# The end of a decoder layer: two expert tiles combined on chip instead of three, row pairs summed by GpSimd, five token tiles finished from PSUM

## The chip, the cores and the metric

The kernel runs on one core of a Trainium2 chip. The metric is the device time of one execution in microseconds (us). The core has five engines: TensorE (PE: matmuls, and PEld for its weight loads), VectorE (DVE), ScalarE (ACT), GpSimd (POOL), and SP, whose queue here issues most DMAs. Each runs its own instructions in program order and waits for the others through semaphores. SBUF is the working memory on chip; matmuls write into PSUM, eight banks of 128 rows by 512 fp32 words.

## What is computed

A decoder layer on 1024 tokens of width 1024: attention, then a mixture of 32 experts in which every token goes through two, then an RMS normalization. Only the end matters here:

```python
y = jnp.zeros_like(xt)
for e in range(N_EXPERTS):
    he = jax.nn.silu(xt @ w_gate[e]) * (xt @ w_up[e])
    y = y + combine[:, e:e + 1] * (he @ w_down[e])     # two nonzero weights per token
...
    x = x + y.reshape(B, T, D)
return _rmsnorm(x, final_norm)
# _rmsnorm(x, g) = x * rsqrt(mean(x * x) + 1e-6) * g
```

## The kernel before

**Experts.** The loop `for e in range(NE)` runs 32 jobs. Job `i = 4q + c` is one expert; the four jobs of group `q` share three row tiles of 128 gathered token rows, `x0`, `xq`, `x1` (numbers `j = 3q, 3q+1, 3q+2`), where `xq` is shared by two experts. A job takes two halves of gate and up projection (`gate_up`, 12 matmuls each, on weights that ACT and DVE split into a high and a low part, `split_half`, L98), the activation (`act_mul`), a transposition (`trans_h`), the down projection (`project`, four matmuls into two `s` banks) and the addition of its result to the row tiles (`add`, DVE). `finish(i)` does the last two and, if `c` is above 0, row tile `j` is complete: for `j < 21` GpSimd scatters its rows into `Y_d` (`scatter`), a table in DRAM with two rows per token, one for each of its experts. The down projection of job `e - 1` runs in the round of job `e`. The order on TensorE, ACT, DVE and GpSimd is the order in which the code is written.

**The last group.** The three row tiles of `q = 7` (j = 21, 22, 23) are not scattered. `finish` splits each into a high and a low part (`yk`, appended to `kept`), and `combine_kept` adds them to a token tile's PSUM banks: one matmul per half, part and kept tile with a one-hot matrix (`hots`, made on DVE by `token_onehot`) that sends each kept row to its token. Job 29's `finish` runs in the round of 31, after the first half of its gate and up; job 28's in round 29.

**The final stage.** `load_y` loads the eight token tiles with both rows per token (`fy`, 1 MB each) through SP's queue; the loads wait for the last scatter. `second_rows(t)` lets ACT copy a tile's second rows into two PSUM banks, `combine_kept` adds the kept rows there, and DVE adds the banks to the first rows (L1070). ACT squares the tile and sums the squares (L1075), takes the root (L1082); DVE takes the reciprocal (L1054) and multiplies by it and by the gain (L1057), and SP stores the tile (L1059). Tile `t - 1` is closed (`finish_out`) after tile `t`'s adds; copies run two tiles ahead, over three pairs of banks. The last tile is squared in two halves (L1080) and its sums added (L1081). Since PSUM banks are written by ACT and then added to by TensorE, a bank that has not been opened by a matmul is first written by one (L1043).

The main lines of the stage:

```python
combine_kept(t, early[t], range(NK - 1 if t < EC else 0, NK))
if t + 2 < NT:
    early[t + 2] = second_rows(t + 2, yys[t + 2])
for n, bk in enumerate(early.pop(t)):
    nc.vector.tensor_tensor(o[:, c], o[:, c], bk, op=ALU.add)
if t:
    finish_out(t - 1)
nc.scalar.activation(yy[:, 1, :], o, AF.Square, accum_out=ss)
```

After it the program reads a count of overflowing experts and, where it is zero, ends.

## Time and profile before

| | |
|---|---|
| median of three timed runs | 1029.95 us (1028.26 to 1030.7) |
| the profiled execution | 1027.5 us |
| its span | 1025.7 us |
| mean granted TensorE clock | 0.994 |
| busy, share of the span | PE 96%, DVE 74%, ACT 61%, GpSimd 10% |
| HBM traffic | 206 GB/s over the span |

The page of a profile covers one execution; its times are in us from the start of the span. The shares are averages over stages with different limits, so a change at the end is read from the last 50 us: from the timeline (instructions in order of time, with what ended the engine's idle time before them in brackets), from the table by stretches and from the chain of waits that ended last. The profiled execution took 1.8 us more than its span.

### The profile page before, as it was taken

How to read it: one execution, taken by the hardware profiler on the slowest of the kernel's cores; microseconds unless marked ns; L12 is line 12 of the kernel's file. 1: busy time of each engine (PE TensorE's matmuls, PEld its weight loads, DVE VectorE, ACT ScalarE, POOL GpSimd, SP SyncE). 2: the span in 40 equal slices, each digit the busy share in tenths (PEclk: the TensorE clock that was granted, in tenths of full speed). 3: DMA queues.
4: the chain of work that ended last, by engine and by line, in shares of the span. 5: the costliest groups of instructions: out<-in, count | busy, mean ns of one | idle time of the engine just before them, and what ended most of it. 6: DMA issues, size and time to landing. Idle time of an engine off the chain costs nothing.

```text
span 1025.7 us, 15824 instructions
## 1 busy us (share of the span) xinstructions
PE 988.3 (96%) x5466; PEld 798.7 (78%) x5466; DVE 758.6 (74%) x1814; ACT 627.2 (61%) x1278; POOL 107.1 (10%) x108
## 2 busy tenths in 40 slices
PE   6999999999999999999999999899999999999995
PEld 5978888988889888998788788776767667666764
DVE  6746686467763677636877568779899898898986
ACT  6557675376764767546766343376666676666655
POOL 0011000010000100000000000111121221131100
PEclk9999999999999999999999999999999999999998
DMA  7994221212121121211738899389999999997364
GB/s 244 270 282 150 63 62 43 63 42 62 42 63 42 42 63 42 63 42 62 228 132 260 270 336 318 126 282 352 370 369 368 365 378 370 366 366 276 136 246 165
DMA packets 151147, 200.45 MB, mean 195 GB/s; under 512 B 14287, under 2 KB 124975, under 8 KB 150041
## 3 DMA queue, kind: packets, MB, share of 16 engines
q1 hardware_dynamic: 144584, 182.71, 54.1%
q0 software_dynamic: 6480, 16.72, 4.5%
q8 instruction: 44, 0.72, 0.3%
q14 instruction: 39, 0.31, 0.1%
HBM read 170.07 MB, written 40.98 MB: 206 GB/s over the span
## 4 chain that ended last, share of the span: by engine, by line
PE 86%; DMA 4%; DVE 4%; ACT 2%; issue 2%; SPq 0%; DVEq 0%; POOL 0%; POOLq 0%; ACTq 0%
PE s L1127 10%; PE pv L410 6%; PE pt L375 6%; PE pj L306 6%; PE pj L308 6%; PE pj L1096 6%; PE pj L1095 6%; PE pj L1097 6%; PE pj L307 6%; PE s L350 3%; PE s L346 3%; PE pj L280 3%; PE pj L281 3%; PE pj L279 3%; PE pt L664 2%
## 5 line engine op out<-in xcount | busy, mean ns | idle before, releaser
L97 ACT ACTIVATE gw<-ring 128x1024 fp32r<-128x1024 f32 x114 | 117.2, 1055 | 63.1 <-PE pj L1097 60.3
L98 DVE TENSOR_TENSOR gw<-ring,gw 128x1024 fp32r<-128x1024 f32 x114 | 134.4, 1219 | 2.0 <-ACT gw L97 1.4
L359 ACT ACTIVATE prob<-prob,nm 128x128 f32<-128x128 f32 (+7 forms) x128 | 99.1, 774 | 53.6 <-DVE nm L353 53.1
L98 DVE TENSOR_TENSOR ptl<-pt,pth 128x512 fp32r<-128x512 f32 (+1 forms) x160 | 96.9, 632 | 28.1 <-ACT pth L97 27.6
L1095 PE MATMUL pj<-gw,xh 128*128 128x512 f32 x256 | 115.4, 451 | 0.1
L97 ACT ACTIVATE pth<-pt 128x512 fp32r<-128x512 f32 (+1 forms) x160 | 84.0, 552 | 39.1 <-PE pt L375 36.4
L1096 PE MATMUL pj<-gw,xh 128*128 128x512 f32 x256 | 101.7, 397 | 0.2
L1097 PE MATMUL pj<-gw,xl 128*128 128x512 f32 x256 | 101.2, 395 | 0.4 <-DVE xl L675 0.4
L306 PE MATMUL pj<-hT,whl 128*128 128x512 f32 x240 | 96.0, 400 | 0.0
L308 PE MATMUL pj<-hT,whl 128*128 128x512 f32 x240 | 95.0, 396 | 0.0
L307 PE MATMUL pj<-hT,whl 128*128 128x512 f32 x240 | 94.8, 395 | 0.0
L353 DVE CUSTOM_DVE_ANT_0 prob<-s,bias 128x512 f32<-128x512 f32 (+3 forms) x128 | 71.8, 568 | 26.9 <-PE s L350 24.8
L410 PE MATMUL pv<-pth,vq 128*128 128x256 f32 x320 | 81.8, 275 | 4.0 <-DVE oT L415 2.2
L375 PE MATMUL pt<-ident,prob 128*128 128x128 f32 x576 | 84.3, 274 | 1.3 <-ACT prob L359 1.3
L410 PE MATMUL pv<-ptl,vq 128*128 128x256 f32 x320 | 80.3, 287 | 0.1
L375 PEld LDWEIGHTS pt<-ident,prob 128*128 128x128 f32 x576 | 67.0, 140 | 13.2 <-DVE ptl L98 3.8
L279 PE MATMUL pj<-whl,hT 128*128 128x256 f32 (+1 forms) x256 | 73.4, 287 | 1.0 <-ACT whl L97 1.0
L280 PE MATMUL pj<-whl,hT 128*128 128x256 f32 (+1 forms) x256 | 73.4, 287 | 0.0
L346 PE MATMUL s<-k,q 128*128 128x512 f32 (+2 forms) x192 | 72.4, 379 | 1.1 <-DVE nm L353 1.1
L281 PE MATMUL pj<-whl,hT 128*128 128x256 f32 (+1 forms) x256 | 73.3, 286 | 0.0
L1127 PE MATMUL s<-rd,ht 128*128 128x512 f32 x160 | 71.9, 592 | 0.0
L350 PE MATMUL s<-k,q 128*128 128x512 f32 (+2 forms) x192 | 70.7, 369 | 0.0
(359 smaller groups left out, 2231.5 us busy)
## 6 DMA issues: line engine op xcount, KB each, us to landing
ring<-in_w_expert_gate SPq DMA_DIRECT2D x57, 512.0 KB, 7.9
ring<-in_w_expert_up SPq DMA_DIRECT2D x57, 512.0 KB, 7.0
rd<-in_w_expert_down SPq DMA_DIRECT2D x20, 1024.0 KB, 8.0
wraw<-in_w_in SPq DMA_DIRECT2D x24, 512.0 KB, 4.3
Y_d<-zeros SPq DMA_DIRECT2D x8, 1024.0 KB, 8.6
rdx<-in_w_expert_down SPq DMA_DIRECT2D x8, 1024.0 KB, 8.6
fy<-Y_d SPq DMA_DIRECT2D x8, 1024.0 KB, 5.9
G_d<-R_d SPq DMA_DIRECT2D x8, 576.0 KB, 8.5
```

What stands on the lines that cost most here:

```text
L97: ins = nc.scalar.activation(hi, src, AF.Copy)
L98: (eng or nc.vector).tensor_tensor(lo, src, hi, op=ALU.subtract)
L279: nc.tensor.matmul(bk[:, :n], hTh(kt)[:, tk], hi[:, k, :], start=(kt == 0), stop=False)
L306: nc.tensor.matmul(bk, hi[:, kt, :], hTh(kt)[:, c], start=(kt == 0), stop=False)
L307: nc.tensor.matmul(bk, lo[:, kt, :], hTh(kt)[:, c], start=False, stop=False)
L308: nc.tensor.matmul(bk, hi[:, kt, :], hTl(kt)[:, c], start=False, stop=(kt == KT - 1))
L375: nc.tensor.transpose(tp[:, o:o + P], pr[qq][:, kb * P:(kb + 1) * P], ident)
L410: nc.tensor.matmul(pv[:, o0:256], vq[:, kb, vh, :], pp[:, kk * 256:kk * 256 + w], start=(kb == 0 and i == 0), stop=(diag and kk == 1 and i ...
L1095: nc.tensor.matmul(gu, ah, wh, start=(kt == 0), stop=False)
L1096: nc.tensor.matmul(gu, ah, wl, start=False, stop=False)
L1097: nc.tensor.matmul(gu, al, wh, start=False, stop=(kt == KT - 1))
L1127: nc.tensor.matmul(bks[n], ht[:, j * P:(j + 1) * P], rd[:, j, n * 512:(n + 1) * 512], start=(j == 0), stop=(j == 1))
```

## The change

`NK` goes from 3 to 2: row tile 21 is scattered like those before it, and only 22 and 23 are kept. Job 29's `finish` moves from round 31 into round 30, and job 30's and 31's down projections stand one behind the other, with job 31's transposition between the two halves of the former. `load_y` waits for one scatter more.

A string `KIND` gives each token tile one of three ways. "I" (tiles 0 and 7) is the old way. "P" (1, 2, 3, 4, 6): GpSimd adds the second rows to the first, ACT copies the sum into PSUM, the kept rows are added there, ACT squares both halves straight out of PSUM, and DVE's closing multiply reads PSUM too; the adds of DVE fall away. "S" (5): GpSimd adds the rows, the kept rows stand alone in PSUM and DVE adds them as before. Tiles in two halves need their two sums added by DVE before the root. There are four pairs of banks instead of three, one of them mixed (`s`, `pv`), and copies run three tiles ahead, after the root of a tile. Banks of pairs 0 and 3 are opened by a matmul on one-hot data before ACT overwrites them.

```diff
--- before.py
+++ after.py
@@ -50,7 +50,8 @@
 BT = 8
 ORD = ((0, 1, 2, 3), (1, 2, 3, 0))
 F7 = 41
-NK = 3
+NK = 2
+KIND = "IPPPPSPI"
 SP = 1
 OL0 = (20, 21, 22, 23)
 OL1 = (20, 21, 22, 23)
@@ -1034,14 +1035,20 @@
             for i in ks:
                 for q in range(2):
                     nc.tensor.matmul(bk, hots[i // 2][:, i % 2, t], kept[i][:, q, n * 512:(n + 1) * 512],
-                                     start=False, stop=(i == NK - 1 and q == 1), skip_group_check=True)
+                                     start=(KIND[t] == "S" and i + q == 0), stop=(i == NK - 1 and q == 1),
+                                     skip_group_check=True)
 
     def second_rows(t, yy):
-        bks = [(b_pt, b_pj, b_s)[t % 3]() for _ in range(2)]
-        for n, bk in enumerate(bks):
-            if t == 0:
-                nc.tensor.matmul(bk, hots[0][:, 0, t], kept[0][:, 0, n * 512:(n + 1) * 512], start=True, stop=True)
-            nc.scalar.activation(bk, yy[:, 1, n * 512:(n + 1) * 512], AF.Copy)
+        bks = [bk() for bk in ((b_pt, b_pt), (b_pj, b_pj), (b_s, b_s), (b_s, b_pv))[t % 4]]
+        if KIND[t] != "I":
+            nc.gpsimd.tensor_tensor(yy[:, 0, :], yy[:, 0, :], yy[:, 1, :], op=ALU.add)
+        if KIND[t] != "S":
+            k = int(KIND[t] == "I")
+            for n, bk in enumerate(bks):
+                if t % 4 in (0, 3):
+                    mark = hots[0][:, n, 0:4].rearrange("p t c -> p (t c)")
+                    nc.tensor.matmul(bk, hots[0][:, 0, 0], mark, start=True, stop=True)
+                nc.scalar.activation(bk, yy[:, k, n * 512:(n + 1) * 512], AF.Copy)
         return bks
 
     def final(yys, combine):
@@ -1052,34 +1059,41 @@
         def finish_out(t):
             o, ss = yys[t][:, 0, :], sss[t]
             nc.vector.reciprocal(ss, ss)
-            halves = [slice(0, D)] if t < NT - 1 else [slice(0, 512), slice(512, D)]
-            for c in halves:
-                (nc.gpsimd if t in PL and combine else nc.vector).scalar_tensor_tensor(
-                    o[:, c], o[:, c], ss, gain_l[:, c], op0=ALU.mult, op1=ALU.mult)
+            whole = [slice(0, D)]
+            halves = [slice(0, 512), slice(512, D)]
+            bks = early.pop(t, None)
+            for n, c in enumerate(halves if bks or t == NT - 1 else whole):
+                src = bks[n] if bks else o[:, c]
+                nc.vector.scalar_tensor_tensor(o[:, c], src, ss, gain_l[:, c], op0=ALU.mult, op1=ALU.mult)
+            for c in halves if t == NT - 1 else whole:
                 nc.sync.dma_start(out[t * P:(t + 1) * P, c], o[:, c])
 
         sss = []
         for t, yy in enumerate(yys):
             o = yy[:, 0, :]
             if combine:
-                combine_kept(t, early[t], range(NK - 1 if t < EC else 0, NK))
-                if t + 2 < NT:
-                    early[t + 2] = second_rows(t + 2, yys[t + 2])
-                for n, bk in enumerate(early.pop(t)):
+                if t >= EC:
+                    combine_kept(t, early[t], range(NK))
+                if KIND[t] != "P":
+                    for n, bk in enumerate(early.pop(t)):
+                        c = slice(n * 512, (n + 1) * 512)
+                        nc.vector.tensor_tensor(o[:, c], o[:, c], bk, op=ALU.add)
+            ss = mo.tile([P, 1], F32, tag="fss", name="fss", bufs=3)
+            bks = early.get(t)
+            if bks or t == NT - 1:
+                s2 = [mo.tile([P, 1], F32, tag="fs2", name="fs2", bufs=4) for _ in range(2)]
+                for n in range(2):
                     c = slice(n * 512, (n + 1) * 512)
-                    nc.vector.tensor_tensor(o[:, c], o[:, c], bk, op=ALU.add)
+                    nc.scalar.activation(yy[:, 1, c], bks[n] if bks else o[:, c], AF.Square, accum_out=s2[n])
+            else:
+                nc.scalar.activation(yy[:, 1, :], o, AF.Square, accum_out=ss)
             if t:
                 finish_out(t - 1)
-            ss = mo.tile([P, 1], F32, tag="fss", name="fss", bufs=3)
-            if t < NT - 1:
-                nc.scalar.activation(yy[:, 1, :], o, AF.Square, accum_out=ss)
-            else:
-                s2 = [mo.tile([P, 1], F32, tag="gate", name="fs2", bufs=2) for _ in range(2)]
-                for n in range(2):
-                    c = slice(n * 512, (n + 1) * 512)
-                    nc.scalar.activation(yy[:, 1, c], o[:, c], AF.Square, accum_out=s2[n])
+            if bks or t == NT - 1:
                 nc.vector.tensor_tensor(ss, s2[0], s2[1], op=ALU.add)
             nc.scalar.activation(ss, ss, AF.Sqrt, scale=1.0 / D, bias=epsT)
+            if combine and t + 3 < NT:
+                early[t + 3] = second_rows(t + 3, yys[t + 3])
             sss.append(ss)
         finish_out(NT - 1)
 
@@ -1119,9 +1133,11 @@
         nc.scalar.activation(ht, tp[:, :256], AF.Copy)
         return ht
 
-    def project(ht, rd):
+    def project(ht, rd, mid=None):
         bks = []
         for n in range(2):
+            if n and mid is not None:
+                mid()
             bks.append(b_s())
             for j in range(2):
                 nc.tensor.matmul(bks[n], ht[:, j * P:(j + 1) * P], rd[:, j, n * 512:(n + 1) * 512],
@@ -1260,7 +1276,7 @@
             add(bks or project(ht, raw_d.pop(i)), job(i)[1], i == NE - 2)
             if c:
                 y = xgs[j % NX][:, 0:D]
-                if j < 3 * 7:
+                if j < 3 * 8 - NK:
                     sc = scatter(y, dstM[:, RI[c - 1], q:q + 1])
                     if j >= 3 * 7 - HS:
                         hold(sc, queued[-HQ])
@@ -1285,7 +1301,7 @@
             if e == 20:
                 ol_steps = overflow_list()
                 for k in range(NK):
-                    nc.vector.tensor_copy(srcL[:, k:k + 1], srcM[:, RI[k], 7:8])
+                    nc.vector.tensor_copy(srcL[:, k:k + 1], srcM[:, RI[k + 3 - NK], 7:8])
                 nc.vector.tensor_tensor(rel, srcL[:, :, None].to_broadcast([P, NK, NT]),
                                         tok0[:, None, :].to_broadcast([P, NK, NT]), op=ALU.subtract)
             gu = b_pj()
@@ -1293,8 +1309,6 @@
             gs = gate_cols(cols)
             gate_up(gu, c0, 0)
             split_half(2 * e + 2)
-            if e == NE - 1:
-                finish(e - 2, ht)
             if e:
                 ht = trans_h(hms.pop(e - 1))
             tps = None
@@ -1314,7 +1328,7 @@
                 split_half(2 * e + 3)
             if e in OL1:
                 next(ol_steps, None)
-            if 0 < e < NE - 2:
+            if 0 < e < NE - 1:
                 finish(e - 1, ht)
             if tps and EV == 2:
                 evac_x(tps[1], j, 1)
@@ -1324,20 +1338,17 @@
                 split_half(2 * e + 3)
         yys = load_y()
         nc.scalar.activation(warm, warm, AF.Sqrt)
+        h31, ahead = [], []
+        down30 = project(ht, raw_d.pop(NE - 2), lambda: h31.append(trans_h(hms.pop(NE - 1))))
         early[0] = second_rows(0, yys[0])
-        ahead = []
-
-        def last_down():
-            h31 = trans_h(hms.pop(NE - 1))
-            combine_kept(0, early[0], (0,))
-            ahead.append(project(h31, raw_d.pop(NE - 1)))
-
-        finish(NE - 2, ht, between=last_down)
+        finish(NE - 2, None, down30, lambda: ahead.append(project(h31[0], raw_d.pop(NE - 1))))
         early[1] = second_rows(1, yys[1])
-        combine_kept(1, early[1], (0,))
-        combine_kept(0, early[0], (1,))
+        for t in range(EC):
+            combine_kept(t, early[t], (0,))
         finish(NE - 1, None, ahead[0])
-        combine_kept(1, early[1], (1,))
+        early[2] = second_rows(2, yys[2])
+        for t in range(EC):
+            combine_kept(t, early[t], (1,))
         gain_l = rdp.tile([P, D], F32, tag="rd", name="gain_l", bufs=4)
         with after(queued[-1]):
             nc.sync.dma_start(gain_l, bc_rows(final_norm, D))
...
```

On DVE, in rounds 30 and 31 (`gw` are the split weights, `xg` the row tiles, `sg` the activation). Before, from the activation of job 30:

```order
L1111 SCALAR_TENSOR_TENSOR sg<-sg,gate,pj 128x256
L1281 TENSOR_TENSOR oh<-io,rel 128x1024
L98 TENSOR_TENSOR gw_6644<-ring,gw_6644 128x1024 x2
L1104 TENSOR_SCALAR gate<-xg_7770,firstM 128x1
L1139 TENSOR_TENSOR xg_7768<-xg_7768,s 64x512 x2
L1141 SCALAR_TENSOR_TENSOR xg_7769<-xg_7769,firstM,s 64x512 x2
L98 TENSOR_TENSOR yk<-xg_7768,yk 128x512 x2
L1111 SCALAR_TENSOR_TENSOR sg<-sg,gate,pj 128x256
```

The same place in the changed kernel:

```order
L1125 SCALAR_TENSOR_TENSOR sg<-sg,gate,pj 128x256
L1155 TENSOR_TENSOR xg_7768<-xg_7768,s 64x512 x2
L1157 SCALAR_TENSOR_TENSOR xg_7769<-xg_7769,firstM,s 64x512 x2
L1297 TENSOR_TENSOR oh<-io,rel 128x1024
L99 TENSOR_TENSOR gw_6644<-ring,gw_6644 128x1024 x2
L1118 TENSOR_SCALAR gate<-xg_7770,firstM 128x1
L1125 SCALAR_TENSOR_TENSOR sg<-sg,gate,pj 128x256
```

The four additions of job 29 now stand ahead of the weight splits for job 31's second half, and the difference of tile 21 is gone.

On ACT, from the transposed activation of job 31 into the final stage (`pt`, `pj`, `s`, `pv` are banks, `fy` the token tiles, `fs` a half's sum). Before:

```order
L1119 ACTIVATE ht<-pv 128x256
L97 ACTIVATE yk<-xg_7769 128x512 x2
L1044 ACTIVATE pj<-fy 128x512 x2
L97 ACTIVATE yk<-xg_7770 128x512 x2
L1044 ACTIVATE s<-fy 128x512 x2
L1075 ACTIVATE fy,fss<-fy 128x1024
L1082 ACTIVATE fss<-fss,epsT 128x1
L1044 ACTIVATE pt<-fy 128x512 x2
L1075 ACTIVATE fy,fss<-fy 128x1024
```

In the changed kernel, where `pj<-fy` reads what GpSimd has added:

```order
L1133 ACTIVATE ht<-pv 128x256
L1051 ACTIVATE pt<-fy 128x512 x2
L98 ACTIVATE yk<-xg_7769 128x512 x2
L1051 ACTIVATE pj<-fy 128x512 x2
L98 ACTIVATE yk<-xg_7770 128x512 x2
L1051 ACTIVATE s<-fy 128x512 x2
L1089 ACTIVATE fy,fss<-fy 128x1024
L1094 ACTIVATE fss<-fss,epsT 128x1
L1051 ACTIVATE s<-fy 128x512
L1051 ACTIVATE pv<-fy 128x512
L1087 ACTIVATE fy,fs_10549<-pj 128x512
L1087 ACTIVATE fy,fs_10550<-pj 128x512
```

The copies of tiles 0 and 1 stand in the same places relative to the kept tiles, but tile 0's now come after the transposition, and tile 1 is squared in two halves out of its banks.

On DVE at the end, from tile 5's adds (`fy<-fy,pj`) on, in the changed kernel:

```order
L1093 TENSOR_TENSOR fss<-fs_10620,fs_10621 128x1
L1080 TENSOR_TENSOR fy<-fy,pj 128x512 x2
L1061 RECIPROCAL fss<-fss 128x1
L1067 SCALAR_TENSOR_TENSOR fy<-pt,fss,gain_l 128x512 x2
L1061 RECIPROCAL fss<-fss 128x1
L1067 SCALAR_TENSOR_TENSOR fy<-fy,fss,gain_l 128x1024
L1093 TENSOR_TENSOR fss<-fs_10662,fs_10663 128x1
L1080 TENSOR_TENSOR fy<-fy,s 128x512
L1080 TENSOR_TENSOR fy<-fy,pv 128x512
L1061 RECIPROCAL fss<-fss 128x1
L1067 SCALAR_TENSOR_TENSOR fy<-s,fss,gain_l 128x512 x2
L1093 TENSOR_TENSOR fss<-fs_10682,fs_10683 128x1
```

Before, every tile had the same three steps there, two adds, a reciprocal and one multiply of 1024; now the last tile's sum stands behind tile 6's two closing multiplies.

## Rows read from the trace of the kernel before

**Rows 1.** Chain that ended last, by time: start us, us, engine and line.
```profile
995.49 0.49 DVE fy L1070
...
1014.11 1.28 DVE fy L1057
```

**Rows 2.** Table by stretches: us; busy PE, PEld, DVE, ACT, POOL; clock, DMA.
```profile
1000.00:1005.00 5.00, 5.00 (x23) 4.14 (x23) 4.93 (x9) 4.93 (x11) 0.00 (x0) 1.00 0.52 210
```

**Rows 3.** Timeline, ACT and DVE around tiles 1 to 3: start us, us, engine, line, out<-in.
```profile
999.30 1.04 ACT L1075 ACTIVATE fy<-fy 128x1024 f32<-128x1024 f32 x1
...
999.78 1.28 DVE L1070 TENSOR_TENSOR fy<-fy,s 128x512 f32<-128x512 f32 x2
...
1000.47 0.29 ACT L1082 ACTIVATE fss<-fss,epsT 128x1 f32<-128x1 f32 x1
1000.67 1.10 ACT L1044 ACTIVATE pj<-fy 128x512 f32<-128x512 f32 x2
1000.98 0.15 DVE L1054 RECIPROCAL fss<-fss 128x1 f32<-128x1 f32 x1
1001.17 1.28 DVE L1057 SCALAR_TENSOR_TENSOR fy<-fy,fss,gain_l 128x1024 f32<-128x1024 f32 x1
1001.71 1.05 ACT L1075 ACTIVATE fy<-fy 128x1024 f32<-128x1024 f32 x1
...
1002.37 1.28 DVE L1070 TENSOR_TENSOR fy<-fy,pt 128x512 f32<-128x512 f32 x2
```

**Rows 4.** Timeline, ACT and DVE, the last token tile.
```profile
1013.44 0.63 ACT L1080 ACTIVATE fy<-fy 128x512 f32<-128x512 f32 x1 [0.51 <-DVE fy L1070]
...
1014.59 0.19 ACT L1080 ACTIVATION_READ_ACCUMULATOR fy<-fy 128x1 f32 x1
1015.32 0.15 DVE L1081 TENSOR_TENSOR fss<-fs,fs 128x1 f32<-128x1 f32 x1
...
1015.50 0.29 ACT L1082 ACTIVATE fss<-fss,epsT 128x1 f32<-128x1 f32 x1 [0.72 <-DVE fss L1081]
1015.83 0.16 DVE L1054 RECIPROCAL fss<-fss 128x1 f32<-128x1 f32 x1 [0.36 <-ACT fss L1082]
1016.03 1.41 DVE L1057 SCALAR_TENSOR_TENSOR fy<-fy,fss,gain_l 128x512 f32<-128x512 f32 x2
```

**Rows 5.** Timeline, round 31: gate/up begins; job 29's projection and last additions.
```profile
974.29 0.39 PE L1095 MATMUL pj<-gw,xh 128*128 128x512 f32 x1
...
977.16 3.60 PE L1127 MATMUL s<-rd,ht 128*128 128x512 f32 x8
...
981.51 1.43 DVE L1141 SCALAR_TENSOR_TENSOR xg<-xg,firstM,s 64x512 f32<-64x512 f32 x2
```

**Rows 6.** Timeline: scatter, Y loads; landing times of their line; table by stretches.
```profile
959.40 1.71 POOL L1144 DMA_INDIRECT Y_d<-xg,dstM  x1 [8.27 <-DVE xg L1141]
...
962.89 0.81 SPq L1026 DMA_DIRECT2D fy<-Y_d  x2
...
DMA to landing us min/median/max: 4.9/5.9/6.8
...
980.00:982.50 2.50, 2.50 (x12) 1.73 (x11) 1.94 (x4) 1.53 (x3) 0.00 (x0) 1.00 1.02 429
```

**Rows 7.** GpSimd group by form (count, busy, mean ns); timeline, DVE beside GpSimd.
```profile
L98 POOL TENSOR_TENSOR whl<-wraw,whl 128x1024 fp32r<-128x1024 f32 x10 | 23.9, 2392 | 209.6 <-PE s L350 142.0 <-ACT whl L97 47.1 <-PE s L348 20.2
...
148.78 0.61 POOL L321 CAST q<-q 64x512 fp32r<-64x512 f32 x1 [7.72 <-DVE q L318]
148.98 1.49 DVE L98 TENSOR_TENSOR whl<-wraw,whl 128x1024 fp32r<-128x1024 f32 x1 [0.27 <-ACT whl L97]
...
171.87 1.23 DVE L98 TENSOR_TENSOR whl<-wraw,whl 128x1024 fp32r<-128x1024 f32 x1 [0.26 <-ACT whl L97]
...
878.65 2.34 DVE L98 TENSOR_TENSOR gw<-ring,gw 128x1024 fp32r<-128x1024 f32 x2
879.00 2.88 POOL L1144 DMA_INDIRECT Y_d<-xg,dstM  x1 [0.45 <-DVE xg L1141]
```

More of the change, by code (lines that the diff above doesn't have):

```diff
@@ L1353, in hymba_layer @@
             nc.vector.tensor_tensor(y, kept[i][:, 0].bitcast(F32), kept[i][:, 1].bitcast(F32), op=ALU.add)
-            scatter(y, dstM[:, RI[i], 7:8])
+            scatter(y, dstM[:, RI[i + 3 - NK], 7:8])
         o16 = tri[:, 0:NO]
```

## The prediction, made before the changed kernel was run

> **What bounds the kernel now.** TensorE is busy 96% of the span, but the change touches only what follows expert 30, so I read that stretch alone. The chain of waits is on TensorE until 995.49, then on VectorE (DVE) until tile 6's closing multiply at 1014.11 [rows 1]: the final stage, eight token tiles summed, normalized and stored. The table by stretches shows how close its two engines are: from 1000 to 1005 both DVE and ScalarE (ACT) are busy 4.93 of 5.00 us [rows 2]. The timeline gives the pace. DVE takes 2.59 us per tile: two adds 1.20, reciprocal 0.19, closing multiply 1.20 [rows 3]. ACT takes 2.41 us: a Square of 1024 with its accumulator read 1.17, a square root 0.20, two copies into PSUM 1.04 [rows 3]. So DVE sets the pace, with ACT only 0.18 us per tile behind it. That gap is the number to keep in mind.
>
> **The change part by part.** The profiled execution took 1027.5 us, 1.8 more than its span of 1025.7; the median of the three timed runs, 1029.95, is 2.45 above it. I work out shifts of the last reciprocal, now at 1015.83 [rows 4]; what follows it (two multiplies, the last stores, the end of the program) stays as it is.
>
> (a) When the final stage can start. Row tile 21 is now scattered, and every Y load waits for that scatter. Its down projection moves ahead of expert 31's first half of gate/up, which began at 974.29, and takes 3.60 to the end of its last matmul; DVE needs some 2.0 more for three of its four pieces of addition (1.43 for the last two) [rows 5]: 979.9. The previous scatter was issued at 959.40, about 0.3 after the addition that fed it, and the loads were released at 962.89, 3.49 later [rows 6]. That gives 980.2 and 983.7. A load lands 4.9 us after issue at the earliest, and at 429 GB/s a megabyte takes 2.45 [rows 6]: tile 0 at 988.6, tile 1 at 991.1, tile 7 at about 1006. Before, two loads were issued at 962.89 and were there by about 970; no load was waited for. Tile 1 now goes through a GpSimd add first; the nearest row, a subtraction of the same size there, takes 2.39 [rows 7]: 993.6. ACT works in program order, and behind tile 1's copies stands the splitting of the last kept tile, which all the remaining combining matmuls need. Copies 1.04, two split passes priced like them 1.04, DVE's second difference priced as half an add pair 0.64, and 0.4 of matmuls and handovers: the first add starts at 996.7 instead of 995.49, **1.2 us later**. The second half of gate/up of expert 31 also waits about 1.3 us for its weight splits, now queued on DVE behind four more additions; the combining that stood between the projections is gone, so the last projection still ends within half a microsecond of where it did, and both are covered by the wait for tile 1. If the loads came at once, 0.4 of it would show.
>
> (b) The pace. For five tiles (1 to 4 and 6) DVE loses the adds and needs only a sum of two scalars 0.18, a reciprocal 0.19 and two half multiplies 1.41 [rows 3, 4]: 1.8 instead of 2.59. ACT gains nothing on them. Square goes in two halves, 1.15 from the first to the last read, plus 0.19 for that read; then ACT waits while DVE adds the halves, 0.22 with the handovers, and the root follows with 0.20 [rows 3, 4]: 1.76, and with copies 2.80 instead of 2.41. **ACT becomes the bound.** Its work from tile 0's Square to the last reciprocal: tiles 0 and 5 whole, 1.37 each; five tiles at 1.76; four pairs of copies left, 4.16; tile 7's halves 1.34; the last sum and root 0.55. That is 17.6. The Square starts 1.33 after the first add, at 998.0, so with no wait the last reciprocal would stand at 1015.6, where it stands now: what tile 5's missing copies and the earlier ones save, (a) and the halves take back.
>
> (c) Waits that the new order puts on ACT, found by laying these durations along the order of the four engines. Tile 5's adds wait for its matmuls, which stand on TensorE behind the matmuls that open tile 7's banks, and those wait for tile 3's closing multiplies: 0.9. At the end DVE runs tile 7's adds only after tile 6's sum, 0.5, and tile 7's sum only after tile 6's closing multiplies, 0.9. Tile 3's sum waits for tile 2's multiplies, 0.4, and 0.2 falls on smaller ones. Together 2.9, so the last reciprocal comes at 1018.5, **2.7 late**. If half of them hide behind one another it is 1.5, with every one a little longer 3.5.
>
> (d) GpSimd and DVE side by side. Between 991 and 1006 GpSimd adds for 2.39 of every 2.5 us. The trace before has no such add beside a DVE instruction with both inputs in SBUF, but it has two neighbours. A DVE split of 1.23 took 1.49 beside a GpSimd cast of 0.61 that had begun 0.20 earlier; and a GpSimd scatter issue that started 0.35 after two back-to-back DVE splits took 2.88 and ended 0.89 after them, against 1.71 for another [rows 6, 7]. So one holds up the other. On the path of ACT three or four such DVE instructions fall into this stretch: the difference of the last kept tile and the sums of tiles 1 and 2, perhaps 3 (tile 0's closing multiply is a fifth, off the path). Each waits between nothing and one whole add, 0 to 2.39; ends 0 and 9.6. Nearest row, the cast: held for 0.27 of the 0.41 that was left of it. I take half an add, 1.2, three times: **3.6**.
>
> The Trainium skill (SBUF — State Buffer, "Who interferes with whom") says that a DVE instruction with two SBUF inputs contends with a GpSimd instruction that reads SBUF, and that whichever starts first holds the shared ports for its whole length. The trace agrees in kind, with the 1.49 against 1.23. Taken to the letter, with four holds laid along the order, an estimate would be 4.9 for this term instead of 3.6.
>
> The fewer combining matmuls (eight per tile instead of twelve) save TensorE time where it waits anyway: nothing. One token one-hot on DVE less: nothing, since TensorE leads there. On SP's queue the final gain's load now stands ahead of the waiting Y loads, and behind them only the stores, which need the tiles anyway; on GpSimd's queue nothing stands behind the six adds but the end of the program. Both at nothing; were a store held up, it would be by the next tile's 2.8.
>
> Sum: 2.7 + 3.6 = 6.3 us. On the profiled execution 1033.8; on the median of the runs shown 1036.2.
>
> **Rivals.** No holding: GpSimd and DVE read side by side for these shapes. For it: that row's DVE instruction was only 0.27 longer, and two of the three on the path are 128x1, whose reading takes next to no time. Against: a short instruction still has to get in. Then (a) to (c) stand alone: +2.7, 1032.6 (1031.5 to 1034).
>
> Not slower: ACT's order hides the waits, and tile 1's add is no longer what it waits for. The place is the start of the stage: if tile 1 lands by 989 the split of the last kept tile follows the last projection, and the first add stands at 995.4; with no waits on ACT the 17.6 then end at 1014.3, 1.5 early (1028.4). It becomes faster than can be measured from the point where a Square half out of PSUM takes 0.1 us less than one out of SBUF (ten of them, 1.0 more: 1027.4). Against it: the scatter is a chain of four rows, none of which has slack, and (c) is in the order itself. A middle outcome, half of (c) and no holding, gives +1.2: 1031.2, no change that counts.
>
> Worse: the scatter's issue is itself held by the one-hot and two splits that DVE runs right behind it, as in the row with 2.88 [rows 7]; the loads start up to 2.4 later, and each later microsecond moves the first add: 1037.4 to 1038.6, with full holds past 1041.
>
> That the change does not do what it says can be left out: the order shows the six adds on GpSimd and the five tiles' Squares out of PSUM.
>
> **How the numbers follow.** Holding as in (d), 1033.6 to 1040.5: 0.46. No holding, above 1032: 0.20. Beyond 1040.5: 0.08. Within 0.2% (1027.9 to 1032.0, about what a measurement of this kernel can tell from no change): 0.16. Faster: 0.10. Slower is the sum of the first three, 0.74. The likeliest is 1036.2. The range leaves out what lies past 1040.5 and most of the faster case, 0.08 and about 0.09: 1028.5 to 1040.5.
>
> **What would show it.** In the timeline of the changed kernel: Y loads released near 983.7, all eight in a row; six GpSimd adds, one per landed tile, from 991 to 1006; the first DVE add near 996.7; ACT, not DVE, busy near 4.9 of 5.00 afterwards; the closing multiplies of the last tile near 1022. Holding shows as sums of 128x1 that start or end with a GpSimd add, or as differences well over 0.7. If the loads land before 986 or the first add stands before 995.5, (a) is wrong; if a PSUM Square half is under 0.5, (b); if ACT has no idle before tile 5's and tile 7's Squares, (c); if no DVE instruction is late while GpSimd adds, (d), and the time is then near 1032.6. A time under 1028 would mean that ACT is not the bound.

## The result and the profile after

The changed kernel took **1038.24 us** (median of six runs, 1037.55 to 1040.19) against 1029.11 for the kernel before, six runs taken beside it (1026.62 to 1031.46): a ratio of 1.0087, 95% interval 1.007 to 1.0105. The profiled execution took 1037.55 us, its span 1035.8, against 1027.5 and 1025.7.

I compare profiles by one landmark that the change does not touch: the start on TensorE of the transposes of expert 29, at 971.11 before and 974.03 after. The final stage is then measured by two distances from it, to DVE's first addition and to the last reciprocal.

| | transposes of expert 29 | to the first addition | to the last reciprocal | end of the execution |
|---|---|---|---|---|
| before | 971.11 | 24.38 | 44.72 | 1027.5 |
| after | 974.03 | 29.47 | 51.51 | 1037.55 |

The two landmarks (before, then after) and the last reciprocal after (that of before is the 1015.83 of [rows 4]; the first additions are the 995.49 of [rows 1] and the 1003.50 below):

```profile
971.11 0.38 PE L1117 MATMUL pv<-ident,sg 128*128 128x128 f32 x2
...
974.03 0.38 PE L1131 MATMUL pv<-ident,sg 128*128 128x128 f32 x2
...
1025.54 0.16 DVE L1061 RECIPROCAL fss<-fss 128x1 f32<-128x1 f32 x1 [0.36 <-ACT fss L1094]
```

So of the 10.05 us between the two profiled executions 6.79 arise in the tail, 2.92 had been lost before the landmark, and 0.34 come after the last reciprocal.

Three excerpts show the tail of the changed kernel. First the timeline (start us, us, engine, line, out<-in, idle time and releaser in brackets) from the scatter to the first tiles; L99 is the differences of the kept tiles, L1044 the GpSimd additions, L1080 the additions of the final stage, L1067 the closing multiplies, L1093 the sums of two halves.

```profile
981.76 0.98 POOL L1160 DMA_INDIRECT Y_d<-xg,dstM  x1 [17.73 <-DVE xg L1155]
...
985.00 4.08 SPq L1027 DMA_DIRECT2D fy<-Y_d  x8
...
992.34 15.81 POOL L1044 TENSOR_TENSOR fy<-fy 128x1024 f32<-128x1024 f32 x6 [9.61 <-PE pt L1050]
...
993.92 4.10 DVE L99 TENSOR_TENSOR yk<-xg,yk 128x512 fp32r<-128x512 f32 x2 [0.51 <-ACT yk L98]
998.05 1.41 DVE L1157 SCALAR_TENSOR_TENSOR xg<-xg,fA,s 128x512 f32<-128x512 f32 x2
999.50 4.08 DVE L99 TENSOR_TENSOR yk<-xg,yk 128x512 fp32r<-128x512 f32 x2
...
1000.87 0.73 PE L1037 MATMUL pt<-yk,oh 128*128 128x512 f32 x2 [0.85 <-DVE yk L99]
...
1003.50 1.40 DVE L1080 TENSOR_TENSOR fy<-fy,pt 128x512 f32<-128x512 f32 x2
...
1003.63 0.54 PE L1037 MATMUL pt<-yk,oh 128*128 128x512 f32 x1 [2.04 <-DVE yk L99]
...
1006.70 2.54 DVE L1067 SCALAR_TENSOR_TENSOR fy<-fy,fss,gain_l 128x1024 f32<-128x1024 f32 x1
1009.16 0.15 DVE L1093 TENSOR_TENSOR fss<-fs,fs 128x1 f32<-128x1 f32 x1
```

Counted from the landmark, the scatter and the loads come some 19 us later than those of [rows 6]. The six additions fill GpSimd from 992.34 to 1008.15, 2.64 each where [rows 7] has 2.39. Beside them a pair of differences takes 4.10 and 4.08; in the kernel before it was 1.28 and 1.48:

```profile
989.15 1.28 DVE L98 TENSOR_TENSOR yk<-xg,yk 128x512 fp32r<-128x512 f32 x2
...
992.96 1.48 DVE L98 TENSOR_TENSOR yk<-xg,yk 128x512 fp32r<-128x512 f32 x2
```

Taken one by one, the halves of the first pair last 1.33 and 2.85 and those of the second 1.32 and 2.84, instead of some 0.68 each; TensorE, which waits for the second pair, is released by its halves at 1000.87 and 1003.63. The closing multiply of tile 0 takes 2.54 instead of 1.28 [rows 3]. Another kind of DVE instruction stands there nearly untouched: the two additions of 1003.50 (one input in PSUM), 1.40 against 1.28. The first sum of two halves, 1009.16, comes when GpSimd is done, and takes 0.15.

The same view of ACT in the steady part, tile 2 finished in PSUM, and of the Square of tile 5:

```profile
1009.34 0.29 ACT L1094 ACTIVATE fss<-fss,epsT 128x1 f32<-128x1 f32 x1 [0.64 <-DVE fss L1093]
1009.54 1.10 ACT L1051 ACTIVATE pt<-fy 128x512 f32<-128x512 f32 x2
1010.58 0.57 ACT L1087 ACTIVATE fy<-s 128x512 f32<-128x512 f32 x1
1011.06 0.19 ACT L1087 ACTIVATION_READ_ACCUMULATOR fy<-s 128x1 f32 x1
1011.15 0.58 ACT L1087 ACTIVATE fy<-s 128x512 f32<-128x512 f32 x1
1011.63 0.19 ACT L1087 ACTIVATION_READ_ACCUMULATOR fy<-s 128x1 f32 x1
1012.05 0.29 ACT L1094 ACTIVATE fss<-fss,epsT 128x1 f32<-128x1 f32 x1 [0.23 <-DVE fss L1093]
...
1019.28 1.06 ACT L1089 ACTIVATE fy<-fy 128x1024 f32<-128x1024 f32 x1 [1.12 <-DVE fy L1080]
```

From root to root it is 2.71, with 0.23 of waiting: the 2.59 of DVE and 2.41 of ACT per tile [rows 3] have become 2.7 of ACT. The table by stretches (us; busy PE, PEld, DVE, ACT, POOL; granted clock; DMA), to be held against [rows 2]:

```profile
1000.00:1005.00 5.00, 2.12 (x7) 1.43 (x7) 4.86 (x4) 1.14 (x4) 5.00 (x3) 0.89 1.01 421
1005.00:1010.00 5.00, 5.00 (x19) 3.99 (x18) 3.01 (x5) 4.32 (x11) 3.15 (x2) 0.76 0.29 120
1010.00:1015.00 5.00, 2.98 (x14) 2.13 (x12) 3.57 (x9) 4.13 (x14) 0.00 (x0) 1.00 0.54 218
```

In the first stretch DVE is "busy" 4.86 of 5.00, and about half of that is waiting inside the differences (the pair of 999.50 takes 2.60 more than its 1.48 before); ACT is down to 1.14, TensorE to 2.12, and the granted clock, 1.00 (2.4 GHz) until then, is 0.89 and then 0.76 on the mean, parts of these stretches at 1.2 GHz. Later neither DVE nor ACT is full: 3.57 and 4.13 of 5.00.

### The profile page after: what moved, and what is told of

Same layout as the page of the kernel before. It is cut to its first block, busy times and chain, and to the rows that moved or that the text cites. A ratio compares the mean times of both kernels' runs of the same rounds, so it can differ in the third digit from the quotient of the medians.

```text
span 1035.8 us, 15787 instructions
## 1 busy us (share of the span) xinstructions
PE 990.1 (96%) x5440; PEld 797.2 (77%) x5440; DVE 759.0 (73%) x1810; ACT 626.2 (60%) x1284; POOL 124.3 (12%) x115
## 5 line engine op out<-in xcount | busy, mean ns | idle before, releaser
L99 DVE TENSOR_TENSOR gw<-ring,gw 128x1024 fp32r<-128x1024 f32 x114 | 134.4, 1219 | 3.1 <-ACT gw L98 2.5
L99 DVE TENSOR_TENSOR ptl<-pt,pth 128x512 fp32r<-128x512 f32 (+1 forms) x160 | 96.9, 632 | 28.6 <-ACT pth L98 28.1
```

Of the source, the lines that this page charges most:

```text
L99: (eng or nc.vector).tensor_tensor(lo, src, hi, op=ALU.subtract)
```

## The experiments

All kernels below by the same landmark; the times are medians, each beside its own runs of the kernel before (1028.5 to 1029.1), and left out where only one execution was taken.

| kernel | landmark | first addition | last reciprocal | time |
|---|---|---|---|---|
| before, two more profiles (e6, e11) | 971.84, 970.72 | 24.40, 24.39 | 44.73, 44.73 | |
| after, one more profile (e10) | 972.94 | 29.59 | 52.59 | |
| e1: no GpSimd additions | 975.73 | 24.41 | 47.19 | 1033.26 |
| e2: all tiles the old way | 974.95 | 24.42 | 44.75 | 1030.28 |
| e3: GpSimd only writes | 975.85 | 24.41 | 47.73 | 1032.95 |
| e4: tiles 1 and 2 the old way | 975.00 | 26.26 | 50.95 | 1036.13 |
| e5: before, with four GpSimd additions | 972.14 | 26.70 | 47.13 | 1031.07 |
| e7: tile 7 opened later | 975.34 | 29.63 | 50.49 | 1035.5 |
| e8: only the last tile in PSUM | 974.69 | 24.40 | 44.66 | 1030.22 |
| e9: e1 and e7 together | 971.04 | 24.41 | 44.58 | |

The final stage of the kernel before repeats within 0.02 us (44.72, 44.73, 44.73), while the landmark moves by 5 over all profiles; so the distances can tell kernels apart that the times do not. The changed kernel's own two profiles, however, differ by 1.08 (51.51 and 52.59): there a difference of a microsecond between two single profiles does not yet tell two kernels apart.

**e1, the additions taken away.**

```diff
-        if KIND[t] != "I":
-            nc.gpsimd.tensor_tensor(yy[:, 0, :], yy[:, 0, :], yy[:, 1, :], op=ALU.add)
```

> The changed kernel without the six GpSimd additions; the second rows of tiles 1 to 6 are left out of the sums. Everything else, the late scatter and the new order included, stays. Theory (holding): the two pairs of differences of the kept tiles, 4.10 and 4.08 us in the changed kernel, fall back to 1.28 each, the first addition of the final stage comes about 5.6 us earlier counted from the transposes of expert 29, and the time is 5.5 to 6.5 us lower than that of the changed kernel (1038.2), near 1032. Rival (the differences are long for another reason, such as the Y loads that write SBUF at some 420 GB/s at the same time): they stay near 4.1 and the time stays above 1036.5.

The timeline of DVE, and ACT and TensorE at tile 5:

```profile
995.62 1.29 DVE L99 TENSOR_TENSOR yk<-xg,yk 128x512 fp32r<-128x512 f32 x2 [0.51 <-ACT yk L98]
...
998.49 1.47 DVE L99 TENSOR_TENSOR yk<-xg,yk 128x512 fp32r<-128x512 f32 x2
1000.14 1.29 DVE L1078 TENSOR_TENSOR fy<-fy,pt 128x512 f32<-128x512 f32 x2 [0.17 <-PE pt L1037]
...
1012.48 3.47 PE L1037 MATMUL pj<-yk,oh 128*128 128x512 f32 x8
...
1016.72 1.06 ACT L1087 ACTIVATE fy<-fy 128x1024 f32<-128x1024 f32 x1 [2.55 <-DVE fy L1078]
```

Both pairs are back at 1.29 and 1.47, the first addition stands 24.41 from the landmark as in the kernel before, and the stage is 4.32 us shorter. I had expected more: 5.6 for the first addition (it is 5.06) and 5.5 to 6.5 for the time (4.98); part is lost again at tile 5, before whose Square ACT waits 1.43 longer than in the changed kernel. The loads ran at 419 to 433 GB/s beside these differences too, so they are not what lengthens them. What is left, 47.19 against 44.72, is the new way of finishing: ACT waits 2.55 for tile 5's additions, and these for combining matmuls of which eight take 3.47 here and 2.00 in the changed kernel; the granted clock of that stretch, 1010 to 1015, is 0.76 (partly 1.2 GHz), after TensorE had been busy 3.12 of the 5 us before.

**e2, everything but the finishing.**

```diff
-KIND = "IPPPPSPI"
+KIND = "IIIIIIII"
```

> The changed kernel with all eight token tiles finished the old way (no GpSimd addition, no tile finished in PSUM); two kept tiles, the late scatter and the four bank pairs stay. Theory: scatter and bank pairs alone are about neutral; without GpSimd additions the first addition comes near where it was in the kernel before, the stage runs at 2.6 us per tile, and from the transposes of expert 29 to the last reciprocal it is 44.0 to 45.0 us (44.72 before, 51.51 in the changed kernel). The time is then 1028 to 1030 if the 2.9 us that the changed kernel lost at the start of the expert loop are not there, 1031 to 1033 if they are there again. Rival (the late scatter and the wait for the Y loads cost several us themselves): 47 us or more in that stretch.

44.75: the late scatter, two kept tiles and four bank pairs alone cost the tail nothing and bring it nothing. The time, 1030.28, is 1.001 of the kernel before (0.9991 to 1.0029).

**e3, GpSimd as busy, without reading.**

```diff
-            nc.gpsimd.tensor_tensor(yy[:, 0, :], yy[:, 0, :], yy[:, 1, :], op=ALU.add)
+            for _ in range(3):
+                nc.gpsimd.memset(yy[:, 0, :], 1.0)
```

> The changed kernel with each GpSimd addition replaced by three GpSimd writes of a constant over the same half of the tile (tiles 1 to 6 do not hold the reference's sums). GpSimd is as busy at the same places, but reads no tensor. Theory (it is GpSimd's reading of SBUF beside a DVE instruction with two SBUF inputs that holds): differences 1.28 per pair as without the additions; time about 1 to 2 us above the run without additions, because tile 1 still waits for GpSimd: 1032 to 1034.5. Rival (any GpSimd access to SBUF, writing too, holds DVE): differences of 3 us or more per pair and a time above 1036.

```profile
994.24 17.56 POOL L1045 MEMSET fy<- 128x1024 f32 x18 [9.67 <-PE pt L1051]
...
995.74 1.29 DVE L99 TENSOR_TENSOR yk<-xg,yk 128x512 fp32r<-128x512 f32 x2 [0.51 <-ACT yk L98]
...
997.24 1.12 ACT L1052 ACTIVATE pj<-fy 128x512 f32<-128x512 f32 x2 [1.01 <-POOL fy L1045]
...
998.94 1.29 DVE L99 TENSOR_TENSOR yk<-xg,yk 128x512 fp32r<-128x512 f32 x2 [0.25 <-ACT yk L98]
```

Eighteen writes fill 17.56 us beside both pairs, longer than the six additions, and both pairs take 1.29. So it is not GpSimd's being at work, nor its writing, that holds DVE. The stage is 0.54 longer than in e1, less than the 1 to 2 expected: ACT's copies of tile 1 do wait 1.01 for GpSimd (997.24), yet the first addition stands at 24.41. The Trainium skill (SBUF — State Buffer, "Who interferes with whom") states it so: a DVE instruction with two SBUF inputs contends with a GpSimd instruction that reads SBUF and not with one that only writes it, and one with at most one SBUF input, outside DVE's 2-port modes, does not contend. The trace agrees in all three: 4.10 beside additions, 1.29 beside writes, and 1.40 for a pair of additions out of PSUM.

**e5, the additions put into the kernel before.** `y` is the row tile of expert 30, `junk` a tile that nobody reads.

```diff
                     if i == NE - 2:
+                        junk = rdp.tile([P, D], F32, tag="rd", name="junk", bufs=4)
+                        for _ in range(4):
+                            nc.gpsimd.tensor_tensor(junk, y, y, op=ALU.add)
                         between()
```

> The kernel before, unchanged but for four GpSimd additions of 128x1024 (results used nowhere), put in so that they start when the rows of expert 30 are complete, that is beside the differences of the last two kept tiles. Theory (holding): they take some 10 us in a row from about 988; the two pairs of differences take about 4 us each instead of 1.28 and 1.48, the first addition of the final stage comes 3 to 5.5 us later, and so does the end: 47.5 to 50 us from the transposes of expert 29 to the last reciprocal (44.72 in the kernel before), a time 3 to 5.5 us above it (1028.5), 1031.5 to 1034. Rival (the long differences of the changed kernel belong to its own order or to the loads beside them): both pairs stay under 2, the time within 1 us.

```profile
989.58 8.79 POOL L1271 TENSOR_TENSOR junk<-xg 128x1024 f32<-128x1024 f32 x4 [27.43 <-DVE xg L1141]
...
990.19 4.12 DVE L98 TENSOR_TENSOR yk<-xg,yk 128x512 fp32r<-128x512 f32 x2
...
995.80 3.12 DVE L98 TENSOR_TENSOR yk<-xg,yk 128x512 fp32r<-128x512 f32 x2
998.84 1.35 DVE L1070 TENSOR_TENSOR fy<-fy,pt 128x512 f32<-128x512 f32 x2
```

The differences grow to 4.12 and 3.12 (1.28 and 1.48), with the order and the loads of the kernel before: the holding is settled from both sides. Of the 4.48 us, 2.41 reach the last reciprocal and 2.0 the time (1.0017, interval 1.000 to 1.0034), less than the 3 to 5.5 expected; in the kernel before DVE had waited 0.97 for the projection between the pairs and 1.06 for the combining matmuls before the first addition, and these two, 2.03 together, take up nearly all the rest.

**e4, the additions moved behind the differences.**

```diff
-KIND = "IPPPPSPI"
+KIND = "IIIPPSPI"
```

> The changed kernel with tiles 1 and 2 finished the old way too, so that the first GpSimd addition is that of tile 3 and starts after the differences of the kept tiles. Theory (holding falls on whatever DVE instruction with two SBUF inputs stands beside an addition): both pairs of differences at 1.28, the first addition of the stage some 5 us earlier than in the changed kernel, but the closing multiplies of tiles 0 to 2 out of SBUF take 1.28 to 2.6 each; from the transposes of expert 29 to the last reciprocal 48.0 to 50.0 us (51.51 in the changed kernel), time 2 to 3.5 us under it. Rival (no holding of multiplies, only of differences): 45 to 46.5 us, time 5 to 6 us under it.

```profile
997.75 3.58 DVE L99 TENSOR_TENSOR yk<-xg,yk 128x512 fp32r<-128x512 f32 x2
...
998.42 5.16 POOL L1044 TENSOR_TENSOR fy<-fy 128x1024 f32<-128x1024 f32 x2 [14.71 <-ACT yk L98]
...
1007.99 3.49 DVE L1067 SCALAR_TENSOR_TENSOR fy<-fy,fss,gain_l 128x1024 f32<-128x1024 f32 x1
...
1019.69 1.06 ACT L1089 ACTIVATE fy<-fy 128x1024 f32<-128x1024 f32 x1 [2.71 <-DVE fy L1080]
```

Neither theory's number came for the stage. Tile 3's addition began at 998.42, between the two halves of the second pair, and that pair still takes 3.58; the closing multiply of tile 1 takes 3.49 instead of 1.28, so multiplies are held too, and ACT waits 2.43 for the sum that stands behind it; and tile 5's Square waits 2.71. With 50.95 it gains 0.56, where I had counted on 1.5 to 3.5, and that is less than what lies between the two profiles of the changed kernel. The time is 2.1 lower, within the expected 2 to 3.5, but its interval (1.0044 to 1.01 of the kernel before) overlaps that of the changed kernel. I had put the first addition after the differences by the order of loads, and it came one half too early.

**e7 and e9, the wait before tile 5.** e9 is this without the GpSimd additions.

```diff
                 if t >= EC:
                     combine_kept(t, early[t], range(NK))
+                if t == 5:
+                    early[7] = second_rows(7, yys[7])
...
-            if combine and t + 3 < NT:
+            if combine and t + 3 < NT - 1:
```

> The changed kernel with one move in its order: tile 7's banks are opened after tile 5's combining matmuls instead of before them, so that these no longer stand behind tile 3's closing multiplies on TensorE. Theory (that wait is on the path): ACT's idle time before tile 5's Square, 1.12 us in the changed kernel, goes to 0.3 or less, and from the transposes of expert 29 to the last reciprocal it is 50.3 to 50.8 us (51.51 in the changed kernel); time 0.7 to 1.2 us lower, within the scatter of the runs. Rival (ACT's own work follows so closely that another wait takes its place): 51.2 to 51.6.

> The changed kernel without the six GpSimd additions (the second rows of tiles 1 to 6 are left out) and with tile 7's banks opened after tile 5's combining matmuls. Without the additions alone the stretch from the transposes of expert 29 to the last reciprocal was 47.19 us, and ACT stood idle 2.55 us before tile 5's Square. Theory (that wait is the larger part of what finishing in PSUM costs): the idle time goes under 0.3 and the stretch is 44.8 to 45.8 us. Rival (ACT's own work is the bound and the wait only hides other waits): 46.4 or more.

Tile 5's Square in e7, right behind the copies, with no idle time before it:

```profile
1019.07 0.58 ACT L1051 ACTIVATE pv<-fy 128x512 f32<-128x512 f32 x1
1019.59 1.05 ACT L1091 ACTIVATE fy<-fy 128x1024 f32<-128x1024 f32 x1
```

In the changed kernel the idle time of 1.12 is gone and the stage is 1.02 shorter (50.49), as expected; since its two profiles lie as far apart, it is the idle time that carries this reading. The 1035.5 us agree, but cannot be told from 1038.2 as closely. Without the additions the move gives 2.61: 44.58, slightly under the expected 44.8 to 45.8. So, by one profile of a kernel that leaves the second rows out, this wait was all that finishing in PSUM cost beside the holding, and without both the new way is worth 0.14 us against the old one. What DVE saves per tile, ACT spends.

**e8, only the last tile in PSUM.** `KIND = "IIIIIIIP"` instead.

> The changed kernel with tiles 0 to 6 finished the old way and only tile 7 summed by GpSimd and finished in PSUM, the one place where DVE's two additions stand at the end of everything. Theory: the single GpSimd addition comes long after the differences of the kept tiles, so these stay at 1.3 and 1.5; at the end the two additions of tile 7 drop out and its sum and two half multiplies stay; 43.5 to 44.3 us from the transposes of expert 29 to the last reciprocal (44.74 with all eight tiles the old way, 44.72 before). Time 0.4 to 1.2 us under that of all tiles the old way (1030.3), so 1029 to 1030, the same as the kernel before within the scatter. Rival (the addition holds up a closing multiply by 1 us or more on the path): 44.7 or more.

```profile
1013.49 0.60 ACT L1051 ACTIVATE s<-fy 128x512 f32<-128x512 f32 x1 [1.89 <-POOL fy L1044]
```

44.66, between the 43.5 to 44.3 of the theory and the rival's 44.7: the single addition (1010.77, 2.69 us) lets the differences be, 1.29 and 1.47, but what the end saves is lost again before it. ACT waits 1.89 for the addition before it copies tile 7, ahead of tile 5's Square in its order, and the closing multiply beside the addition takes 2.00 instead of 1.28. 1030.22 us, 1.0005 of the kernel before (0.9986 to 1.0024): no gain.

**e6, e10 and e11, the 2.92 us before the landmark.** TensorE, ACT and GpSimd run the same instructions there in the same order in both kernels; DVE has a one-hot of 128x1024 and a cast of 128x1 fewer in the changed one, and one difference of 128x16 instead of 128x24.

> The kernel before once more, for a second profile. From the transposes of the first row tile to the first gate/up matmul it took 1.13 us in the first profile (669.93 to 671.06); in the changed kernel 3.03 and in four relatives of it 2.95, 2.97, 2.97 and 2.20. Theory 1 (that start-up loss belongs to the program as built): 1.1 to 1.3 us again. Theory 2 (it varies from run to run): 2 us or more is as likely. The final stage: 44.5 to 45 us from the transposes of expert 29 to the last reciprocal by either.

> The changed kernel once more, for a second profile. The transposes of expert 29 began at 974.03 in the first profile and at 974.7 to 975.9 in six relatives of it, at 971.11, 971.84 and 972.14 in three builds of the kernel before. Theory 1 (a program built like the changed kernel reaches the tail later): 973.5 to 976 again. Theory 2 (chance): under 973 is as likely. The final stage by either: 51.3 to 51.7 us from there to the last reciprocal.

> The kernel before, for a third profile. Theory 1 (the build sets when the tail is reached): transposes of expert 29 at 970.8 to 972.5. Theory 2 (chance): over 973.5 is as likely. The final stage by either: 44.7 us.

TensorE from the transposes of the first row tile to the first gate/up matmul, in the changed kernel:

```profile
669.69 1.06 PE L665 MATMUL pt<-ident,xg 128*128 128x128 f32 x8 [0.47 <-DMA xg<-X_d,srcF]
672.72 0.64 PE L1109 MATMUL pj<-gw,xh 128*128 128x512 f32 x1 [1.97 <-issue]
```

and in e6, the kernel before:

```profile
667.45 1.04 PE L664 MATMUL pt<-ident,xg 128*128 128x128 f32 x8
670.33 0.47 PE L1095 MATMUL pj<-gw,xh 128*128 128x512 f32 x1 [1.84 <-issue]
```

The pause is there in both (ACT, which empties the transposes' bank, starts 2 us late while nothing in the profile holds it), half of it in e4, and it is absent in the first and third profile of before, in e5, e8 and e9, and in the second profile of after: 1.10 to 1.14 us there. Where it falls the clock falls too (0.83 on the mean from 670 to 680 in the changed kernel's first profile, 1.00 in that of the kernel before), and the way on to the landmark is 301.3 to 301.7 us instead of 300.1 to 300.2. So it is no property of the changed kernel. The routing stage ahead of it moves by up to 6 us from profile to profile as well. Builds like the kernel before reached the landmark at 970.7 to 972.1 (four), those like the changed kernel at 971.0 to 975.9 (nine): they overlap, yet the second lot is later on the whole. Theory 1's range falls with e10's own 972.94 and with e9's 971.04. But the profiles come from several chips, and among those of one chip the builds like the changed kernel are the later ones each time: 975.34 and 974.69 against 972.14 and 971.84 (e5 to e8), 972.94 and 971.04 against 970.72 (e9 to e11). Whether the build has a share in the rest stays open.

e10's tail missed its 51.3 to 51.7: 52.59. Up to the first addition it agrees (29.59); later tile 5's Square waits 2.04 instead of 1.12, with a clock of 0.66 in that stretch:

```profile
1019.24 1.06 ACT L1089 ACTIVATE fy<-fy 128x1024 f32<-128x1024 f32 x1 [2.04 <-DVE fy L1080]
```

In both profiles of the changed kernel TensorE had just waited 2.55 for tile 3's closing multiplies; in the first the clock stayed at 1.00 (1015 to 1020), here it fell. What decides that stays open.

## Why the prediction was right, and where it was not

The sign, the range and the main mechanism held: 1038.24 in 1028.5 to 1040.5, and 6.8 us of tail where I had 6.3 (7.9 in the second profile). The likeliest time, 1036.2, is 2.0 short. Step by step, with times of the changed kernel shifted by the 2.92 where they stand beside predicted ones:

**(a) failed, +1.2 predicted, 0.0 measured.** In every kernel without GpSimd reading beside the differences the first addition stands 24.40 to 24.42 from the landmark, 24.38 before. I let the scatter wait for three of four additions; it went after two (978.8 instead of 980.2), the loads were released at 982.1 instead of 983.7, and the copies of tile 0 followed at 992.23, right behind ACT's copy of the transposes (991.95, 0.38). Tile 1's copies, behind its GpSimd addition, began at 991.8 instead of 993.6, and the splitting of the last kept tile waited for the last projection's additions on DVE and not for them. What delay is left is hidden: without holding the last pair of differences starts 0.9 later than before (22.76 in e1, 21.85 before, from the landmark), and DVE's wait for the matmuls behind it falls from 1.06 to 0.17.

**(b) and (c), +1.5 after the first addition; +2.44 in e1.** The term was mis-sized in one place. From first addition to last reciprocal it is 20.34 before, 22.78 in e1 and 22.04 in the changed kernel. The pace was right: 2.71 per tile against 2.80 (2.09 where no copies fall), a Square half out of PSUM 0.58, and ACT the bound, though busy 4.13 of 5.00 and not near 4.9: its waits for DVE's sums are part of the 2.71. The wait before tile 5's Square, put at 0.9, was 1.12 in the changed kernel, but 2.55 in e1, 2.71 in e4 and 2.04 in e10, where the combining matmuls ran at the lower clock; the sum took TensorE as running at full clock after its pauses. With that wait removed e9 needs 20.17 from first addition to last reciprocal; the work without waits was put at 18.9 (17.6 and the 1.33 to the first Square), so the other waits come to 1.2 where I had 2.0, if the work is as priced. (a) to (c) together: 2.7 predicted, 2.47 in e1. That is luck, two errors that cancel.

**(d), 3.6 predicted, 4.32 measured against e1 (51.51 less 47.19), 5.91 between e7 and e9 (50.49 less 44.58).** The mechanism was right, place and count were not, and the term was too small. I had three or four instructions held for half an addition each, two of them sums of 128x1. Those sums met no addition: the first falls at 1009.16, after GpSimd's last. The differences of both kept tiles were held instead, that of expert 30 too, which I had not counted, since expert 31's additions stand behind it on DVE. And both halves of a pair were held, the second longer than the first: 2.82 and 2.60 more per pair. Tile 0's closing multiply, which I had put off the path, held up tile 1's sum: ACT waits 0.64 before that root, 0.23 in e1. Of the 5.1 by which the first addition comes later than in e1, 0.7 seems to be given back in the rest of the stage; that is e1's longer wait at tile 5 again, at the lower clock. Between e7 and e9, where neither waits there, the 5.22 at the first addition become 5.91 at the end.

**The rivals.** Without holding I had 1032.6; e1, which is that case, took 1033.26. Part of this agreement is luck: e1 is 4.8 above the runs of the kernel before beside it, not 2.7, while its tail is 2.47 longer. "Not slower" had as its condition a first addition where it was: in the kernels without holding that came true, and in e1 ACT's waits alone still made the tail longer. The later scatter of the worst case did not happen: its issue took 0.98, not 2.88.

**Outside the sum.** That the stretch before the tail stays as it is held only within some 5 us of one profiled execution, and going from one execution's time to the median by adding 2.45 was not safe either: after, the median is 0.69 above the profiled run. The first adds 2.92 and the second takes back 1.76; with 0.5 in the tail and 0.34 after the last reciprocal that makes the 2.0. Part of the 2.92 may not be chance: each timed kernel built from the changed one is slower than the kernel before by 0.7 to 2.3 us more than its tail is longer (changed kernel 2.3, e2 1.8, e8 1.2; some 0.3 of it comes after the last reciprocal), and e5, built from the kernel before, by 0.4 less. No experiment here isolates this, and e2 and e8 alone are not clear of the scatter.

## What to carry to other kernels

Work given to GpSimd is not free beside DVE: look at what DVE runs in that stretch, and count each instruction with two SBUF inputs as waiting for the rest of an addition, one by one, even when two of them stand back to back. A DVE instruction with one input in PSUM, or GpSimd writing without reading, can stand there. And measure a small edit at the end of a long kernel by the distance from an untouched landmark: in the kernel before it repeats to hundredths where the time repeats to microseconds. Take a second profile of the changed kernel too; here the distance itself moved by 1.08.

## What the runs showed of the hardware

- GpSimd gets in between two back-to-back DVE instructions: a pair of 1.28 takes 4.10, 1.33 for the first and 2.85 for the second, while the additions themselves only grow from 2.39 to 2.64.
- The price depends on when an addition begins: in e4 an addition that began 0.67 after the first of two differences cost the pair 2.3 us.
- TensorE's clock falls after some waits of the tail: a granted clock of 0.76 in the changed kernel (1005 to 1010) and of 0.67 in e4 (1000 to 1005), each after TensorE had waited for DVE (2.04 and 1.80 us). It does not fall after each: a wait of 2.55 was followed by 1.00 in one profile of the changed kernel and by 0.66 in the other. Eight combining matmuls that take 2.00 elsewhere take 3.47 in e1.
- A pause of about 1.9 us at the start of the expert loop, with nothing in the profile to hold ACT, stands in some executions of either kernel and costs another 1.4 us by the clock behind it.
